# New orders and buffer numbers for seven of the nine instruction lists of an NSA and mLSTM decoder step

## The chip, the cores and the metric

The kernel runs on one core of a Trainium2 chip, in one launch. The metric is device time in microseconds (us). Five engines work side by side: TensorE (PE) multiplies matrices, VectorE (DVE), ScalarE (ACT) and GpSimd (POOL) work on elements, SyncE (SP) issues nearly all of the transfers; ACT issues a few. Each engine takes its instructions strictly in the order in which they stand in its list, and waits at an instruction until what it needs is done, so that everything behind it waits too.

## The reference

One inference step of a trunk of two layers, for a prompt of 512 tokens and eight sample sequences with one new token each (520 columns in all), in float32. Each layer adds to the residual what its mixer makes of the normed input:

```python
x = x + mixer_i(rmsnorm(x, w_i))          # i = 0: NSA attention, i = 1: mLSTM
out = W_out(mix(...) * silu(z))           # one input and one output projection for each mixer
```

Layer 0 is native sparse attention: keys and values are compressed by a small network (reading 1,024 cached rows for each sample through a page table), blocks are selected, and a window is attended, each branch with its own gate. Layer 1 is an mLSTM with four heads of 512 channels: a causal convolution, block-diagonal q, k and v, a stabilised matrix memory for each head that is updated and read, a norm for each head and the silu gate z. The outputs are the new hidden rows after a final norm, the new cache rows and windows, and the new memories (one 512 by 512 matrix for each head of each of the eight samples, and one for the prompt), normalisers, maxima and convolution rows.

## The kernel before

The 520 columns are worked in two chunks of 260. Every product with a weight is made of three matmuls with a split of both sides into a high and a low part (`mm3`, L761: high by high, high by low, low by high), so that a weight tile goes through three steps after its load: `load_w` (L777) issues the transfer of `wraw` on SP, ACT (in some places DVE) rounds it to `whi`, and POOL or DVE subtracts to get `wlo`. The first matmul of a tile needs `whi`, the third needs `wlo`.

Nothing is issued as the program text runs. The calls of all engines are recorded and then issued by lists of numbers that stand at the top of the file; that is why every row of the profile has the line L667, the one call in the helper. In the order of the program the lists are CALLS0 (projection to keys and values, compression), CALLS2 (projections to q and to the gate), ORDER0 (attention), CALLS1 (output projection of layer 0, norm of layer 1, projection `xm`, convolution and gates), ORDER1 (the projection `zm` to layer 1's gate, beside it the state steps of head 0), ORDER2 (the mLSTM cell with heads 1 to 3 and the output projection of heads 0 to 2) and CALLS3 (the output projection of head 3, the final norm, the outputs). Beside them MOVED tables name calls that go to another engine than the code says, and SLOTS gives each tile of a pool the number of its buffer. So the tables set the order in each engine's list; what then waits for what follows from the tiles. Pools that are closed hand their memory to later pools, and a load into the new pool waits for all users of the old tiles that lay there.

Four places matter below.

- The start. `x_t` (the input) and `nw` (norm factors, 12 KB) are loaded on ACT's queue, the weight `wraw` of the first projection and the small `b` on SP's. DVE scales this weight by `nw`, and PE's first matmul reads the scaled weight and `x_t`. Further on SP's load of a weight tile waits for a `wlo`, and sixteen cached pages (`praw`) stand behind it.
- The step from attention to the output projection. PE runs the projection as 24 matmuls for each of 8 tiles and 2 chunks, with the `uo` tiles (attention output, split) as moving side. The first two weights `w_o` are there early. SP then loads `x1` (the residual, from `in_xT`) into a pool that lies where attention's tiles lay; the next `w_o` stand behind it in SP's list.
- The end of ORDER1, `head_close` (L2284) for head 0: PE sums with ones over partitions (`t<-sd,ncs` and `t<-pr,ones`), DVE and ACT make a denominator `dn` and a numerator `nm`, DVE squares it to `pr`, and PE sums this. Beside it the last chunks of `zm` are evicted by DVE (`zt<-mm,rr`), and ACT makes their sigmoid (`zsg`, three passes).
- The tail, the output projection of head 3: DVE adds PE's sums to the residual (`x<-x,mm`), gates the head's output (`num<-num,zs`) and makes some of the `wlo` of the weights `in_m_out`.

Of the kernel before, what the change touches and what calls it, by code (L numbers as in the profile page):

```python
# [123 lines left out]
)  # L124
ORDER2 = (
# [42 lines left out]
)  # L168
CALLS0 = (
# [282 lines left out]
        0, 1, 0,  # L452
    ),
    ("fn", "w"): (
        0, 1, 2, 3, 4, 5, 6, 7, 8, 9, 10, 11, 12, 13, 14, 15, 16, 17, 18, 19, 0, 3, 2, 1, 13, 7, 10,
    ),
    ("fn", "sq"): (
        0, 1, 1, 1, 0, 1, 0, 1, 0, 1, 1, 1, 0, 1,
# [2627 lines left out]
```

## Time and profile before

| | us |
|---|---|
| median of 3 runs | 1004.49 (1002.74 to 1004.94) |
| the profiled execution | 1004.64 |
| its span, first to last instruction | 1002.9 |
| busy: PE | 977.8 |
| busy: DVE | 803.4 |
| busy: ACT | 554.9 |
| busy: POOL | 318.3 |

The profiled execution is 1.7 us longer than its span: that part lies outside of the instructions. PE is busy in 97% of the span. "Busy" is no proof that PE does useful work at its best rate, but here an idle stretch of PE and a stretch with a lower granted clock are the only visible losses, and they can be read window by window.

### The profile page before, as it was taken

Reading aid. Unit: us, or ns where it says so; the run is one execution under the profiler, and the core shown is the slowest. Engines: PE = TensorE matmul, PEld = TensorE weight load, DVE = VectorE, ACT = ScalarE, POOL = GpSimd, SP = SyncE. Lnnn points to the kernel's source line nnn. Section 1 sums busy time; section 2 is a strip of 40 time slices with the busy share of each in tenths; the row PEclk is TensorE's granted clock in tenths of the full one; section 3 lists DMA queues with packets and bytes.
Section 4 is the critical chain, followed back from the end, with each engine's and each line's share of the span. In section 5 each row is a group of like instructions: output and inputs, shape, how many; then the busy total and the mean of one; then the engine's idle time right before and its main releaser. Section 6 shows DMA issues by size and latency. Waiting matters only on the chain.

```text
span 1002.9 us, 22660 instructions
## 1 busy us (share of the span) xinstructions
PE 977.8 (97%) x8329; PEld 865.4 (86%) x8329; DVE 803.4 (80%) x1937; ACT 554.9 (55%) x1224; POOL 318.3 (32%) x389
## 2 busy tenths in 40 slices
PE   7999999999999999998999999999999999999998
PEld 5799999899988888788999997999676778777987
DVE  6988886776599988845787897957697899899986
ACT  6646443423588788723426654676566554654543
POOL 1123434431232435621133322243112332533330
PEclk9999999999999999998999999999999999999999
DMA  8755532335344534634644365688898789997733
GB/s 282 246 163 188 194 123 76 116 99 161 110 136 141 158 99 147 210 131 145 220 151 132 129 201 173 247 288 306 276 306 290 254 300 304 304 315 282 229 112 117
DMA packets 123681, 197.20 MB, mean 197 GB/s; under 512 B 16165, under 2 KB 64550, under 8 KB 123314
## 3 DMA queue, kind: packets, MB, share of 16 engines
q1 hardware_dynamic: 117954, 185.39, 56.8%
q10 hardware_dynamic: 5616, 10.36, 2.8%
q8 instruction: 65, 1.06, 0.4%
q14 instruction: 46, 0.38, 0.1%
HBM read 145.99 MB, written 58.10 MB: 203 GB/s over the span
## 4 chain that ended last, share of the span: by engine, by line
PE 83%; DVE 7%; DMA 3%; SPq 2%; ACT 2%; issue 2%; POOL 1%; DVEq 0%; ACTq 0%
PE mm L667 54%; PE s L667 12%; PE t L667 11%; PE d L667 6%; SPq L667 2%; DMA wraw<-in_w_kv 1%; DVE cs L667 1%; DMA wraw<-in_w_o 1%; DVE num L667 1%; DVE plo L667 1%; DVE wlo L667 1%; DMA dk<-in_cache 0%; DMA praw<-in_cache 0%; DMA wraw<-in_m_out 0%; ACT zsg L667 0%
## 5 line engine op out<-in xcount | busy, mean ns | idle before, releaser
L667 PE MATMUL mm<-hhi,whi 128*128 128x260 f32 x928 | 266.1, 287 | 0.2 <-DVE whi L667 0.2
L667 PE MATMUL mm<-hhi,wlo 128*128 128x260 f32 x928 | 262.7, 283 | 0.9 <-DVE wlo L667 0.8
L667 PE MATMUL mm<-hlo,whi 128*128 128x260 f32 x928 | 262.4, 283 | 0.0
L667 PEld LDWEIGHTS mm<-hhi,whi 128*128 128x128 f32 x928 | 174.8, 188 | 3.2 <-issue 1.5
L667 PEld LDWEIGHTS mm<-hhi,wlo 128*128 128x128 f32 x928 | 174.7, 188 | 1.3 <-DVE wlo L667 1.3
L667 PEld LDWEIGHTS mm<-hlo,whi 128*128 128x128 f32 x928 | 174.4, 188 | 1.1 <-issue 0.5
L667 POOL TENSOR_TENSOR wlo<-wraw,whi 128x512 fp32r<-128x512 f32 (+1 forms) x36 | 65.1, 1813 | 135.5 <-DVE whi L667 37.9
L667 DVE SCALAR_TENSOR_TENSOR cs<-t,wk,cs 128x512 f32<-128x512 f32 x128 | 88.8, 742 | 6.8 <-PE t L667 3.6
L667 DVE TENSOR_TENSOR wlo<-wraw,whi 128x1024 fp32r<-128x1024 f32 (+1 forms) x63 | 70.4, 1119 | 17.9 <-ACT whi L667 12.7
L667 ACT ACTIVATE cs<-cs,SBC 128x1024 f32<-128x1024 f32 x64 | 71.5, 1144 | 18.7 <-PE d L667 17.8
L667 ACT ACTIVATE whi<-wraw 128x1024 fp32r<-128x1024 f32 (+1 forms) x59 | 50.7, 864 | 51.8 <-DMA wraw<-in_m_out 14.3
L667 ACT ACTIVATE s<-s,mn 128x256 f32<-128x256 f32 (+3 forms) x128 | 70.5, 555 | 7.7 <-DVE mn L667 4.9
L667 POOL TENSOR_SCALAR s<-s,sm 128x256 f32<-128x256 f32 (+3 forms) x53 | 50.6, 965 | 54.2 <-DVE sm L667 27.5
L667 PE MATMUL mm<-uh,whi 128*128 128x260 f32 x224 | 65.6, 293 | 0.0
L667 PE MATMUL mm<-uh,wlo 128*128 128x260 f32 x224 | 63.4, 283 | 1.9 <-DVE wlo L667 1.9
L667 PE MATMUL mm<-ul,whi 128*128 128x260 f32 x224 | 63.3, 283 | 0.0
L667 DVE CUSTOM_DVE_ANT_0 s<-s,D 128x128 f32<-128x128 f32 (+3 forms) x128 | 58.3, 486 | 5.5 <-PE s L667 4.1
L667 PE MATMUL mm<-uo,whi 128*128 128x260 f32 x256 | 48.8, 293 | 3.8 <-ACT whi L667 3.8
L667 PE MATMUL s<-phi,w1a 128*128 128x256 f32 (+1 forms) x224 | 48.8, 296 | 0.0
L667 DVE TENSOR_TENSOR plo<-praw,phi 128x256 fp32r<-128x256 f32 (+1 forms) x50 | 39.3, 799 | 7.5 <-ACT phi L667 3.4
L667 PEld LDWEIGHTS mm<-uo,whi 128*128 128x128 f32 x256 | 41.5, 198 | 4.2 <-ACT whi L667 4.0
L667 PEld LDWEIGHTS mm<-uh,wlo 128*128 128x128 f32 x224 | 42.2, 188 | 2.1 <-DVE wlo L667 2.1
(503 smaller groups left out, 2571.0 us busy)
## 6 DMA issues: line engine op xcount, KB each, us to landing
cs<-in_state_C SPq DMA_DIRECT2D x64, 512.0 KB, 5.5
o_cs<-cs SPq DMA_DIRECT2D x64, 512.0 KB, 4.5
praw<-in_cache SPq DMA_DIRECT2D x128, 128.0 KB, 3.7
dk<-in_cache SPq DMA_DIRECT2D x128, 128.0 KB, 2.9
wraw<-in_m_in SPq DMA_DIRECT2D x32, 512.0 KB, 3.8
wraw<-in_m_out SPq DMA_DIRECT2D x32, 256.0 KB, 5.3
wraw<-in_w_kv SPq DMA_DIRECT2D x11, 512.0 KB, 3.9
wraw<-in_w_q SPq DMA_DIRECT2D x8, 512.0 KB, 3.4
```

The costliest lines, as they stand in the source:

```text
L667: return f(*[real(x) for x in a], **{n: real(x) for n, x in k.items()})
```

## The change

Only tables change; no function does. CALLS2, ORDER0, MOVED2 and the table of moved calls of ORDER0 stay as they are. CALLS0 differs in 257 of 892 places (up to place 130, and from 475 to 629), CALLS1 in 190 of 701 (the first 220), and ORDER1, ORDER2 and CALLS3 nearly everywhere. In the tables of moved calls, CALLS0 loses three calls and gains five, CALLS1 loses two and gains five, and ORDER1, ORDER2 and CALLS3 each exchange one. SLOTS gets other numbers for some fifteen kinds of tile. The two orders before and after, by their first lines:

```diff
 ORDER1 = (
-    0, 225, 226, 253, 227, 257, 15, 254, 1, 228, 230, 255, 2, 229, 231, 232, 233, 256, 8, 3, 259, 277, 16, 265, 262,
+    253, 0, 254, 257, 1, 2, 225, 226, 227, 15, 228, 229, 30, 274, 230, 231, 232, 233, 255, 265, 8, 3, 4, 256, 16, 5,
...
```

At the start ACT's list now begins with the load of `nw`, ahead of `x_t`; SP's begins with the three loads of the first weight, and the load of `b` stands behind the first cached pages; one of the scalings of this weight is POOL's instead of DVE's; the first rounding of the compression weight (`w1a`, 128x1024) stands behind the rounding `whi` of the projection's weight on ACT; the last load of `x_t` stands two roundings earlier.

The changed file is one line longer, so that L667 is L668 there. In the rows below a number after a name is the tile's own, so that the same name in the same row list means the same tile.

SP at the step from attention to the output projection, before (`dk` are the last rows of the window cache, `x1` is the residual, `wc0` and `wg` belong to layer 1's gates):

```order
L667 DMA dk_6588<-in_vwin 128x8x256
L667 DMA x1_6814<-in_xT 128x1040
L667 DMA wc0_6816<-in_w_qkv 128x192
L667 DMA wraw_6818<-in_w_o 128x1024
L667 DMA x1_6814<-in_xT 128x1040 x2
L667 DMA o_vwin<-in_vwin 16x8176
L667 DMA wraw_6875<-in_w_o 128x1024
L667 DMA wraw_6931<-in_w_o 128x1024
```

And of the change:

```order
L668 DMA dk_6588<-in_vwin 128x8x256
L668 DMA wraw_6789<-in_w_o 128x1024
L668 DMA wraw_6791<-in_w_o 128x1024
L668 DMA x1_6818<-in_xT 128x1040 x2
L668 DMA wc0_6821<-in_w_qkv 128x192
L668 DMA x1_6818<-in_xT 128x1040
L668 DMA wraw_6904<-in_w_o 128x1024
```

Two loads of `w_o` moved ahead of the first load of `x1`. The first of the two waits for a weight tile of a much earlier projection, the second for the `wlo` of the second `w_o` tile.

DVE at the end of ORDER1, before (`t_10326` holds PE's sums, `mm_10243` and `mm_10273` are the last two chunks of `zm`):

```order
L667 TENSOR_TENSOR zt_10315<-mm_10243,rr0_7464 128x260
L667 TENSOR_TENSOR zt_10315<-mm_10273,rr1_7543 128x260
L667 TENSOR_REDUCE dn_10349<-t_10326 128x16
L667 TENSOR_TENSOR dn_10349<-dn_10349,SBC_9038 128x16
L667 TENSOR_TENSOR dn_10349<-dn_10349 128x8
L667 TENSOR_TENSOR dn_10349<-dn_10349,SBC_9038 128x8
L667 RECIPROCAL dn_10349<-dn_10349 128x8
L667 TENSOR_TENSOR nm_10357<-VS_8690,dn_10349 128x32
L667 TENSOR_TENSOR nm_10357<-nm_10357,t_10326 128x32
L667 TENSOR_TENSOR pr_9150<-nm_10357 128x32
```

And of the change (`t_10151` holds the sums, `mm_10263` and `mm_10293` are the last two chunks):

```order
L668 TENSOR_REDUCE dn_10328<-t_10151 128x16
L668 TENSOR_TENSOR dn_10328<-dn_10328,SBC_9038 128x16
L668 TENSOR_TENSOR dn_10328<-dn_10328 128x8
L668 TENSOR_TENSOR zt_10258<-zt_10258,zsg1_10324 128x260
L668 TENSOR_TENSOR zt_10334<-mm_10263,rr0_7463 128x260
L668 TENSOR_TENSOR zt_10334<-mm_10293,rr1_7515 128x260
L668 TENSOR_TENSOR dn_10328<-dn_10328,SBC_9038 128x8
L668 RECIPROCAL dn_10328<-dn_10328 128x8
L668 TENSOR_TENSOR nm_10348<-VS_8690,dn_10328 128x32
L668 TENSOR_TENSOR nm_10348<-nm_10348,t_10151 128x32
L668 TENSOR_TENSOR pr_9144<-nm_10348 128x32
```

On PE the sums into `t` now stand 96 matmuls of `zm` earlier, and with them DVE's first three steps and ACT's step on `dn`, which ACT now does ahead of the last chunk's three sigmoid passes. The five DVE steps from the second product of `dn` to `pr` still stand behind the eviction of the last chunk.

DVE in the tail, before (`x` are residual tiles, `wlo_13139` is the low part of a tile of `in_m_out`):

```order
L667 TENSOR_TENSOR x23_11341<-x23_11341,mm_13051 128x260
L667 TENSOR_TENSOR x23_11341<-x23_11341,mm_13015 128x260
L667 TENSOR_TENSOR x22_11447<-x22_11447,mm_12960 128x260
L667 TENSOR_TENSOR x22_11447<-x22_11447,mm_12977 128x260
L667 TENSOR_TENSOR x24_11290<-x24_11290,mm_13066 128x260
L667 TENSOR_TENSOR x24_11290<-x24_11290,mm_13083 128x260
L667 TENSOR_TENSOR num_12919<-num_12919,zs_12949 128x512
L667 TENSOR_TENSOR num_12915<-num_12915,zs_12949 128x512
L667 TENSOR_TENSOR num_12794<-num_12794,zs_12949 128x512
L667 TENSOR_TENSOR wlo_13139<-wraw_13043,whi_13137 128x512
```

And of the change (`wlo_13121` is the tile that answers to it):

```order
L668 TENSOR_TENSOR x22_11581<-x22_11581,mm_12988 128x260
L668 TENSOR_TENSOR x23_11531<-x23_11531,mm_13004 128x260
L668 TENSOR_TENSOR x24_11284<-x24_11284,mm_13025 128x260
L668 TENSOR_TENSOR x24_11284<-x24_11284,mm_13042 128x260
L668 TENSOR_TENSOR num_12935<-num_12935,hy_12985 128x512
L668 SCALAR_TENSOR_TENSOR num_12935<-CT14_8840,par_7904,num_12935 128x512
L668 TENSOR_TENSOR wlo_13121<-wraw_13058,whi_13104 128x512
L668 TENSOR_TENSOR num_12935<-num_12935,zs_12920 128x512
L668 TENSOR_TENSOR num_13021<-num_13021,zs_12920 128x512
L668 TENSOR_TENSOR num_13019<-num_13019,zs_12920 128x512
```

The low part moved ahead of the three products with `zs`, and two of the six additions to `x` now come later; two other steps on `num` moved ahead of it.

## Rows read from the trace of the kernel before

**Rows 1.** The page's first part: busy time of each engine, its share of the span, its instructions.

```profile
PE 977.8 (97%) x8329; PEld 865.4 (86%) x8329; DVE 803.4 (80%) x1937; ACT 554.9 (55%) x1224; POOL 318.3 (32%) x389
```

**Rows 2.** Busy time by stretches of the span: the stretch, its length, the busy time of PE, of its weight loads, of DVE, ACT and POOL, then the granted clock of TensorE (1.00 is 2.4 GHz, 0.50 is 1.2 GHz), the share of the transfer engines and GB/s.

```profile
0.00:25.00 25.00, 17.71 (x89) 13.14 (x90) 17.42 (x33) 16.57 (x24) 3.12 (x7) 1.00 0.83 281
...
450.00:475.00 25.00, 20.90 (x149) 20.62 (x150) 12.56 (x21) 6.32 (x13) 4.51 (x3) 0.86 0.42 149
...
700.00:725.00 25.00, 22.61 (x198) 18.16 (x198) 15.89 (x50) 11.08 (x28) 5.43 (x12) 0.93 0.81 276
725.00:750.00 25.00, 25.00 (x164) 17.56 (x163) 22.82 (x52) 17.43 (x25) 4.46 (x9) 1.00 0.92 309
...
950.00:975.00 25.00, 22.55 (x185) 21.92 (x184) 21.37 (x50) 9.99 (x22) 7.26 (x8) 1.00 0.47 141
```

**Rows 3.** What PE waited for in the whole span: us in total, how often, the longest.

```profile
PE mm L667 <- DMA wraw<-in_w_kv: 7.2, 1, 7.2
PE mm L667 <- ACT whi L667: 3.8, 1, 3.8
PE mm L667 <- DVE wlo L667: 3.4, 3, 1.9
PE t L667 <- DVE pr L667: 2.4, 1, 2.4
```

**Rows 4.** The timeline of the first 24 us, from the lists of several engines (start, duration, engine, instruction, in brackets the idle time before it and what ended it; ACTq is ACT's issuing of transfers).

```profile
0.79 0.89 ACTq L667 DMA_DIRECT2D x_t<-in_xT  x2
1.71 0.45 ACTq L667 DMA_DIRECT2D nw<-in_norms  x1
...
8.52 0.73 ACT L667 ACTIVATE hhi<-x_t,nw 128x520 fp32r<-128x520 f32 x1 [0.61 <-DMA x_t<-in_xT]
...
6.64 0.49 DVE L667 TENSOR_TENSOR wraw<-wraw,nw 128x128 f32<-128x128 f32 x2 [6.64 <-DMA nw<-in_norms]
...
21.20 1.22 DVE L667 TENSOR_TENSOR wlo<-wraw,whi 128x1024 fp32r<-128x1024 f32 x1
...
7.19 2.10 PE L667 MATMUL mm<-x_t,wraw 128*128 128x260 f32 x4 [7.19 <-DMA wraw<-in_w_kv]
```

**Rows 5.** Transfers of the first 25 us: count, size of each, median us from issue to landing.

```profile
x_t<-in_xT ACTq DMA_DIRECT2D x2, 260.0 KB, 3.8
...
nw<-in_norms ACTq DMA_DIRECT2D x1, 12.0 KB, 4.8
```

**Rows 6.** The step to the output projection: one row of what SP waited for in the whole span, then the timelines of SP, ACT, DVE and PE from 436 to 456.

```profile
SPq L667 <- DVE uo L667: 18.6, 1, 18.6
...
440.77 0.34 SPq L667 DMA_DIRECT2D x<-in_xT  x1
...
443.72 11.27 SPq L667 DMA_DIRECT2D wraw<-in_w_o  x2
...
452.31 1.06 ACT L667 ACTIVATE whi<-wraw 128x1024 fp32r<-128x1024 f32 x1 [12.78 <-DMA wraw<-in_w_o]
...
435.97 1.22 DVE L667 TENSOR_TENSOR wlo<-wraw,whi 128x1024 fp32r<-128x1024 f32 x1
...
453.42 0.59 PE L667 MATMUL mm<-uo,whi 128*128 128x260 f32 x2 [3.80 <-ACT whi L667]
454.68 0.58 PE L667 MATMUL mm<-uo,wlo 128*128 128x260 f32 x1 [0.67 <-DVE wlo L667]
```

**Rows 7.** The end of ORDER1: the timelines of PE and DVE from 714 to 718.

```profile
714.04 0.44 PE L667 MATMUL t<-sd,ncs 128*32 128x8 f32 x32
714.31 0.32 PE L667 MATMUL t<-pr,ones 128*32 128x64 f32 x8
717.02 0.34 PE L667 MATMUL t<-pr,ones 128*32 128x32 f32 x8 [2.39 <-DVE pr L667]
...
714.14 0.43 DVE L667 TENSOR_TENSOR zt<-mm,rr 128x260 f32<-128x260 f32 x1 [1.51 <-PE mm L667]
...
716.06 0.17 DVE L667 TENSOR_TENSOR dn<-dn,SBC 128x8 f32<-128x8 f32 x1 [0.75 <-ACT dn L667]
...
716.78 0.19 DVE L667 TENSOR_TENSOR pr<-nm 128x32 f32<-128x32 f32 x1
```

**Rows 8.** Busy time by shorter stretches, with the columns of rows 2.

```profile
453.00:460.00 7.00, 5.90 (x26) 5.62 (x27) 4.12 (x6) 3.11 (x7) 0.00 (x0) 0.55 0.64 234
...
716.00:720.00 4.00, 2.98 (x18) 1.98 (x18) 3.00 (x17) 1.30 (x6) 0.55 (x2) 0.57 0.66 211
...
955.00:960.00 5.00, 4.24 (x35) 4.24 (x36) 4.83 (x11) 2.37 (x5) 0.76 (x2) 1.00 0.23 69
```

**Rows 9.** The tail: the timelines of DVE and PE from 951 to 957.

```profile
951.20 2.10 DVE L667 TENSOR_TENSOR x<-x,mm 128x260 f32<-128x260 f32 x6
953.22 1.89 DVE L667 TENSOR_TENSOR num<-num,zs 128x512 f32<-128x512 f32 x3
955.02 0.69 DVE L667 TENSOR_TENSOR wlo<-wraw,whi 128x512 fp32r<-128x512 f32 x1
...
956.35 0.75 DVE L667 SCALAR_TENSOR_TENSOR num<-CT,par,num 128x512 f32<-128x512 f32 x1
...
955.76 0.39 PE L667 MATMUL mm<-uh,wlo 128*128 128x260 f32 x1 [1.91 <-DVE wlo L667]
```

**Rows 10.** Transfers from 725 to 950 (a row of the state tiles' loads): count, size of each, median us from issue to landing.

```profile
cs<-in_state_C SPq DMA_DIRECT2D x41, 512.0 KB, 5.5
```

More of the change, by code (lines that the diff above doesn't have):

```diff
@@ L291 @@
 MOVED3 = (
-    2, 12, 16, 23, 27, 30, 31, 35, 65, 69, 120, 124, 141,
+    2, 7, 8, 12, 15, 20, 23, 27, 35, 37, 38, 45, 52, 65, 69, 85, 120, 124, 136, 143, 150,
 )
@@ L301 @@
 MOVEDP1 = (
-    1, 7, 12, 16, 17, 22, 31, 32, 47, 57, 61, 67, 82, 92, 97, 102, 106, 107, 117, 121, 127, 137, 147, 151, 162, 166,
-    172, 177, 181, 182, 196, 197, 211, 212, 230, 244, 246, 248, 328, 335,
+    1, 12, 16, 22, 27, 31, 32, 46, 57, 61, 62, 72, 77, 82, 87, 91, 92, 102, 107, 112, 117, 121, 132, 136, 137, 142,
+    147, 151, 166, 172, 177, 182, 187, 192, 196, 197, 202, 212, 225, 230, 244, 248, 255, 328,
 )
 MOVEDP2 = (
[5 rows of a table removed]
[5 rows of a table added]
 )
@@ L313 @@
     ("wstream", "w"): (
[6 rows of a table removed]
[6 rows of a table added]
     ),
     ("cmpw", "hs"): (
-        0, 1, 0, 1, 0, 0, 1, 0, 1, 0, 0, 1, 0, 1, 0,
+        0, 1, 0, 1, 0, 1, 0, 0, 1, 0, 0, 1, 0, 1, 0,
     ),
     ("ps", "bank"): (
[18 rows of a table removed]
[18 rows of a table added]
     ),
@@ L347 @@
     ("cmpw", "ph"): (
[3 rows of a table removed]
[3 rows of a table added]
     ),
     ("cmpw", "psm"): (
-        0, 1, 2, 2, 1, 0, 2, 1, 0, 2, 1, 0, 2, 1, 0, 2, 0, 1, 2, 1, 0, 1, 2, 1, 2, 0, 1, 0, 2, 1, 2, 1, 0, 1, 2, 2,
-        0, 1, 0, 1,
+        0, 1, 2, 2, 1, 0, 2, 1, 0, 2, 1, 0, 2, 1, 0, 2, 0, 1, 2, 1, 0, 1, 2, 2, 1, 0, 2, 2, 0, 1, 0, 1, 2, 1, 0, 0,
+        2, 1, 2, 1,
     ),
@@ L397 @@
     ("x1n", "sq"): (
-        0, 1, 0, 1, 0, 1, 0, 1, 0, 1, 0, 0, 1, 0,
+        0, 1, 0, 1, 0, 1, 1, 0, 0, 1, 0, 0, 1, 0,
     ),
@@ L402 @@
         29, 30, 31, 32, 33, 34, 35, 36, 37, 38, 39, 40, 41, 42, 43, 1, 0, 4, 2, 6, 5, 8, 9, 19, 22, 27, 25, 33, 31,
[4 rows of a table removed]
[4 rows of a table added]
+    ),
+    ("mi", "cv"): (
+        0, 1, 2, 3, 0, 3, 1, 3, 2, 3, 0, 3, 1, 0, 2, 1, 3, 1, 0, 1, 2, 0, 2, 1, 3, 2, 0, 3, 1, 3, 2, 1,
     ),
@@ L410 @@
     ),
-    ("mi", "cv"): (
-        0, 1, 2, 3, 0, 2, 3, 2, 1, 2, 0, 2, 3, 0, 1, 3, 2, 3, 0, 3, 1, 0, 1, 3, 2, 1, 0, 2, 3, 2, 1, 3,
-    ),
     ("st0", "cse"): (
-        0, 1, 2, 1, 2, 0, 1, 2, 0, 1, 2, 0, 2, 1, 0, 1, 2, 0, 1, 2, 0, 1, 2, 0, 0, 2, 1, 2,
+        0, 1, 2, 2, 1, 0, 1, 2, 0, 1, 2, 0, 1, 2, 0, 1, 0, 2, 1, 2, 0, 2, 1, 0, 1, 0, 2, 0,
     ),
@@ L423 @@
     ("zp", "zsg1"): (
-        0, 1, 1, 0, 1, 1, 1, 0, 0, 1, 1, 0, 1, 0, 1, 1, 0, 1, 1, 0, 0, 1, 0, 1, 1, 0, 1, 0, 1, 0, 1, 0,
+        0, 1, 1, 0, 1, 0, 1, 0, 1, 0, 0, 1, 0, 1, 0, 1, 0, 1, 0, 1, 1, 0, 1, 0, 0, 1, 1, 0, 1, 0, 1, 0,
     ),
     ("st", "cs"): (
-        0, 1, 2, 3, 3, 0, 1, 2, 3, 1, 2, 0, 2, 3, 0, 1, 3, 1, 2, 3, 0, 3, 1, 2, 0, 2, 3, 1, 2, 3, 0, 1, 2, 3, 1, 0,
+        0, 1, 2, 3, 0, 1, 2, 3, 2, 1, 0, 3, 0, 1, 2, 3, 1, 3, 0, 1, 2, 1, 0, 3, 0, 1, 2, 3, 0, 1, 2, 3, 0, 3, 1, 2,
     ),
@@ L434 @@
     ),
+    ("cella", "bd"): (
+        0, 1, 2, 3, 4, 5, 6, 0, 1, 3, 2, 4, 6, 3, 1, 2, 1, 5, 5, 5, 0, 4, 5, 6, 1, 2, 3, 5, 4, 0, 1, 6,
+    ),
     ("cella", "row"): (
-        0, 1, 2, 3, 4, 5, 6, 7, 8, 1, 5, 2, 0, 6, 7, 4, 8, 2, 3, 1, 0, 6, 4, 3, 2, 1, 7, 5, 0, 1, 6, 5, 7, 4, 8, 1,
-        3, 4, 2, 5, 6, 2, 4, 7, 1, 3, 8, 2, 5, 7, 5, 4, 6, 1, 4, 5, 3, 7, 5, 1, 0, 1, 8, 5, 3, 7, 8, 0, 1, 7, 3, 4,
-    ),
-    ("cella", "bd"): (
-        0, 1, 2, 3, 4, 5, 6, 0, 1, 2, 4, 3, 2, 1, 0, 4, 1, 0, 3, 1, 3, 2, 3, 5, 0, 4, 6, 3, 1, 2, 4, 0,
+        0, 1, 2, 3, 4, 5, 6, 7, 8, 3, 2, 1, 4, 7, 0, 3, 2, 1, 4, 5, 2, 3, 5, 4, 2, 3, 5, 4, 7, 3, 2, 4, 7, 1, 8, 3,
+        0, 1, 5, 2, 4, 5, 1, 7, 0, 3, 8, 1, 2, 7, 1, 4, 5, 0, 2, 4, 7, 3, 1, 5, 2, 6, 2, 4, 1, 7, 3, 4, 6, 5, 1, 3,
     ),
     ("cellb", "row"): (
-        0, 1, 2, 3, 4, 5, 0, 2, 1, 3, 5, 2, 1, 0, 4, 1, 2, 0, 3, 5, 4, 0, 2, 3, 1, 0, 2, 4, 5, 3, 0, 4, 3, 2, 1, 2,
-        4, 5, 3, 0,
+        0, 1, 2, 3, 4, 5, 2, 0, 1, 3, 4, 1, 0, 2, 5, 0, 3, 2, 1, 4, 5, 3, 2, 1, 0, 5, 4, 3, 2, 1, 4, 3, 1, 5, 0, 3,
+        1, 2, 4, 5,
     ),
     ("fw", "w"): (
-        0, 1, 2, 3, 4, 5, 1, 0, 2, 1, 0, 5, 3, 4, 0, 5, 3, 1, 2, 4, 5, 0, 1, 2, 4, 0, 5, 1, 4, 2, 0, 3, 4, 2, 5, 0,
-        1, 4, 2, 3, 5, 1, 0, 3, 2, 4, 0, 3, 1, 5, 2, 4, 3, 0, 2, 1, 0, 5, 3, 4, 2, 1, 3, 5, 0, 2, 4, 1, 3, 5, 4, 0,
-        2, 1, 5, 3, 0, 4,
+        0, 1, 2, 3, 4, 5, 1, 0, 3, 1, 5, 4, 2, 0, 1, 3, 2, 4, 5, 0, 3, 2, 1, 5, 0, 2, 3, 4, 2, 5, 0, 1, 4, 0, 3, 4,
+        0, 5, 2, 3, 1, 4, 3, 2, 0, 5, 4, 3, 0, 5, 1, 2, 3, 4, 0, 2, 4, 3, 0, 5, 1, 3, 2, 4, 0, 2, 4, 1, 5, 3, 0, 4,
+        2, 5, 3, 1, 0, 4,
     ),
@@ L454 @@
     ("fn", "w"): (
-        0, 1, 2, 3, 4, 5, 6, 7, 8, 9, 10, 11, 12, 13, 14, 15, 16, 17, 18, 19, 0, 3, 2, 1, 13, 7, 10,
+        0, 1, 2, 3, 4, 5, 6, 7, 8, 9, 10, 11, 12, 13, 14, 15, 16, 17, 18, 19, 0, 7, 5, 10, 3, 15, 13,
     ),
     ("fn", "sq"): (
-        0, 1, 1, 1, 0, 1, 0, 1, 0, 1, 1, 1, 0, 1,
+        0, 1, 1, 0, 1, 1, 0, 1, 1, 0, 0, 0, 1, 0,
     ),
```

321 rows, old and new, of tables (CALLS0, CALLS1, CALLS3, MOVED0) are left out of this document.

## The prediction

> **What bounds the kernel now.** I read four views in this order. The page's first part: PE is busy in 97% of the span, DVE in 80% [rows 1], so the time can fall only where PE waits or is slowed. The busy time by stretches of 25 us: nearly all show PE at 25.00 of 25 with the granted clock at 1.00, as 725 to 750 does; the reader is to see the four that don't [rows 2]. PE stands 7.29 us in the first stretch, 4.10 in that from 450, 2.39 in that from 700, 2.45 in that from 950. Two of them also show a lower clock: 0.86 over 25 us is 0.14 x 25 = 3.5 us of full-rate work lost, 0.93 is 0.07 x 25 = 1.75. Then the list of PE's waits, which names the four holes: the first weight 7.2, `whi` 3.8, `wlo` 3.4 in three waits (the longest 1.9), `pr` 2.4 [rows 3]. Last the timelines around each, for the chain behind it. I call them holes A (start), B (output projection), C (end of ORDER1) and D (tail). Elsewhere PE has nothing to gain from another order; it can only lose there.
>
> **Hole A.** PE starts at 7.19. DVE scales the first weight at 6.64, when `nw` lands, and `nw` was issued at 1.71, behind two loads of `x_t` [rows 4]: 4.9 us on the way, as its own row says (4.8) [rows 5]. Now it is issued first, where `x_t` stood, at 0.79. If its way stays 4.9 us, all moves by 1.71 - 0.79 = 0.9. If it is as quick as the first loads of `x_t`, 3.8 us [rows 5], it lands at 4.6; `x_t`, one issue of 0.45 later, lands at 0.79 + 0.45 + 3.8 = 5.0, and PE gains some 2.1. I take 1.5, between the two. Downstream the start feeds a `wlo` that ends at 21.20 + 1.22, and SP's sixteen pages wait for this tile; ACT's work on the third `x_t` waited for its transfer until 8.52 [rows 4], and that load is issued when it was. If this transfer sets the later steps, nothing is left of the gain: the bound below is 0.
>
> [...]
>
> **Hole B.** SP's load of `x1` stands until 440.77, after 18.6 us of waiting for the last `uo`, and the next `w_o` loads stand behind it; the pair issued from 443.72 reaches ACT at 452.31, 8.6 us later, and PE waits 3.80 for `whi` and 0.67 for `wlo`, 4.47 us [rows 6]. Then the clock is low: 0.55 over 453 to 460 [rows 8], half rate for most of it, the 3.5 us above. In the new order the two loads stand ahead of `x1`. The first waits only for a tile of long before. The second waits for the `wlo` that DVE ends at 435.97 + 1.22 = 437.2 [rows 6]; even with the 8.6 us it lands at 445.8, and with `whi` (1.06) and `wlo` (1.22) it is ready at 448.1. PE's wait began at 453.42 - 3.80 = 449.6, where it wants the first of the two; the second comes 48 matmuls later. So both are in time, and `x1` is not held up, since 437.2 lies before 440.77. What PE needs next, later `w_o` tiles, stands behind `x1` as before, from some 442 on; each has 48 matmuls of time. B gives 4.47 + 3.5 = 8.0. The bounds are 0, if something else is late at 449.6, and 8.0.
>
> **Hole C.** PE ends its `zm` matmuls at about 714.1, runs the sums (714.04 to 714.63), and starts on `pr` only at 717.02 [rows 7]. The chain between is DVE's eviction of the last chunk, three sigmoid passes on ACT with the step on `dn` behind them, and DVE's steps from 716.06 to 716.97. Now the sums and DVE's first steps lie 96 matmuls earlier, and ACT does its `dn` step before the last passes. But DVE's five steps still stand behind the last eviction. So PE waits for 0.43 (eviction, from 714.14) and 716.97 - 716.06 = 0.91 of steps, with the gaps 1.4 us, against 2.39: 1.0 less. The clock: after the 2.39 wait it was 0.57 over 716 to 720; after the wait of 1.91 in the tail it stayed 1.00 over 955 to 960 [rows 8]. A wait of 1.4 is nearer to the second, so I take no fall and 1.75 more. C gives 2.75; the bounds are 0 and 2.39 + 1.75 = 4.1.
>
> [...]
>
> **Hole D.** DVE works without a gap: six additions to `x`, three products with `zs` (1.89), then the `wlo` at 955.02 for which PE waits 1.91 [rows 9]. Now `wlo` stands ahead of the three products and of two additions (2.10 / 6 = 0.35 each), but behind two other steps on `num` (0.75 for one [rows 9], about 0.63 for the other, a third of 1.89). Net 1.89 + 0.70 - 1.38 = 1.2 us earlier. D gives 1.2, bounds 0 and 1.91.
>
> **Everything else.** The same number of matmuls runs, and in the dense stretches DVE, POOL and SP have other orders under a full PE. That cover is thin in places: the state steps from 725 run with the transfer engines at 0.92 [rows 2], and in ORDER2 and the tail some of DVE's steps now stand only a dozen of PE's instructions ahead of their use. Before, waits below a microsecond were what such closeness cost, and rows 3 holds all that mattered. I charge 1.0 for new small waits; the bounds are 0 and what the fourth rival below says.
>
> **Sum.** 1.5 + 8.0 + 2.75 + 1.2 - 1.0 = 12.4. The profiled execution took 1004.64, its span 1002.9 with 1.7 outside, which the change doesn't touch. 1004.64 - 12.4 = 992.2. The median of the runs shown is 1004.49, so the same sum from there gives 992.1; the runs spread from 1002.74 to 1004.94.
>
> **Rivals.**
> 1. Only hole B goes. For it: A's gain is lost to the third `x_t`, C keeps its clock fall, D's list is dense. Against: C's and D's shortening follow from steps with measured durations. 1004.64 - 8.0 = 996.6.
> 2. Hole B is only halved. The early loads share the transfer engines with the last cache windows, or ACT or DVE comes to `whi` and `wlo` late behind `uo`; PE waits for half of 4.47 and the clock falls all the same. B is then worth 2.2, and 1004.64 - (1.5 + 2.2 + 2.75 + 1.2 - 1.0) = 998.0. Against it: the first load has some 20 us (SP stood at `x1` for 18.6).
> 3. Nothing shows. All gains are given back in small waits under the dense stretches: 1004.6. For it only that nearly every list is new; against it 12 us of small waits, where the kernel before had under 3 outside of the four holes.
> 4. Slower. In ORDER2 SP's list holds the loads of state tiles behind stores (`zd` at the end of ORDER1, then `o_cs`), each waiting for a DVE step; a load takes 5.5 us [rows 10] with the transfer engines at 0.92 [rows 2], and PE's sums over a head's tiles (`d<-cs`) come late by one load in heads 1, 2 and 3. With a clock fall of 1.75 each, 3 x (5.5 + 1.75) = 21.8, and 1004.64 - 12.4 + 21.8 = 1014.0. It decides from 12.4 / 3 - 1.75 = 2.4 us of lateness for each head. For it: the high share. Against: before, the same loads and stores under the same share let PE run 25.00 of 25 [rows 2].
>
> **How the numbers follow.** The four holes as summed 0.55; rival 1 0.2; rival 2 0.1; rival 3 0.05; rival 4 0.1. The forecast is the likeliest, 992.2. With all upper bounds, 2.1 + 8.0 + 4.1 + 1.9 = 16.1, the time is 988.5, and a run can lie 1 us below; so 987.5 below. Above, the range takes in rivals 1 and 2 with a few more small waits, to 1001; what is left out is rivals 3 and 4 and little else. A difference under 0.2% (2 us) is about what a measurement of this kernel cannot tell from none. Faster than that: 0.55 + 0.2 + 0.1 = 0.85; within it 0.05; slower 0.1.
>
> **What would show it.** A: PE's first matmul at 5.1 to 6.3, and the `wlo` near 21.2 earlier by as much. B: no wait of PE for `whi` near 445 to 450, SP's `w_o` loads issued before `x1`, and a clock of 1.00 through the following 25 us. C: a wait for `pr` of 1.2 to 1.6 and a clock of 1.00 after it. D: a wait for `wlo` under 1 us. Elsewhere PE at 25.00. Wrong would be a wait for `whi` of over 2 us at B, a clock below 0.95 in any stretch, or PE idle by more than 1 us in one stretch of heads 1 to 3.

## The result and the profile after

| | us |
|---|---|
| before, median of 6 runs of this comparison | 1003.62 (1001.97 to 1008.53) |
| after, median of 6 runs | 997.16 (995.11 to 999.03) |
| ratio | 0.9928, 95% interval 0.9902 to 0.9954 |
| the profiled execution after, and its span | 999.03, 996.5 |

The kernel became faster by 6.5 us in the median. The forecast was 12.4 us of gain, to 992.2, with a range of 987.5 to 1001.0: the direction and the range held, half of the gain did not come. The profiled execution is the slowest of the six after. One correction to the section on the change: CALLS1 gains four moved calls, not five, and ORDER1, ORDER2 and CALLS3 exchange more than one: 12, 46 and 4 numbers leave their tables and 16, 41 and 12 enter. So more work goes to POOL, which is busy 336.3 us after against 318.3 before.

The page's first part after, which answers to [rows 1]:

```profile
PE 973.9 (98%) x8329; PEld 860.4 (86%) x8329; DVE 797.8 (80%) x1922; ACT 556.0 (56%) x1224; POOL 336.3 (34%) x404
```

The busy time by stretches of 25 us after (columns as in [rows 2], the clock third from the end):

```profile
0.00:25.00 25.00, 18.68 (x97) 13.62 (x98) 18.23 (x32) 16.61 (x24) 4.28 (x8) 1.00 0.85 290
150.00:175.00 25.00, 23.02 (x174) 22.11 (x175) 16.89 (x25) 7.60 (x15) 10.65 (x8) 1.00 0.20 65
450.00:475.00 25.00, 25.00 (x211) 25.00 (x210) 17.47 (x28) 9.10 (x21) 7.56 (x6) 1.00 0.52 181
700.00:725.00 25.00, 22.69 (x133) 14.50 (x132) 20.12 (x57) 13.99 (x30) 9.05 (x17) 1.00 0.91 289
850.00:875.00 25.00, 23.66 (x186) 18.92 (x186) 16.71 (x42) 19.43 (x34) 11.47 (x10) 1.00 0.92 318
...
950.00:975.00 25.00, 23.79 (x191) 22.94 (x190) 20.59 (x44) 9.49 (x24) 12.42 (x13) 1.00 0.26 81
```

Hole B is closed, and the clock is at 1.00 in every stretch. But the stretches from 150 and from 850, full before, have holes now. PE's waits after, by what ended them, against [rows 3]:

```profile
PE d L668 <- DMA x_t<-in_xT: 5.7, 2, 5.0
PE s L668 <- DVE plo L668: 3.5, 3, 2.7
PE mm L668 <- DVE wlo L668: 1.4, 2, 0.8
PE t L668 <- DVE VB L668: 1.3, 1, 1.3
PE t L668 <- DVE pr L668: 1.3, 1, 1.3
PE mm L668 <- POOL wlo L668: 1.0, 2, 0.9
...
PE mm L668 <- DVE cs L668: 0.7, 1, 0.7
...
PE mm L668 <- DVE bdm L668: 0.6, 1, 0.6
```

`whi` is gone, `pr` is 1.3 instead of 2.4. New are `plo` with 2.7 in one wait, `VB` with 1.3, `cs`, `bdm` and one of 0.9 for a `wlo` from POOL. The largest new one lies near 152. Timeline of the compression there, after (start, duration, engine, step; in brackets the idle time before it and what ended it):

```profile
147.17 0.69 DVE L668 TENSOR_TENSOR psm<-praw 128x512 f32<-128x512 f32 x1 [0.71 <-DMA praw<-in_cache]
147.78 0.88 DVE L668 SCALAR_TENSOR_TENSOR hs<-hs,hcst,hsg 128x636 f32<-128x636 f32 x1
148.25 2.59 POOL L668 TENSOR_TENSOR plo<-praw,phi 128x1024 fp32r<-128x1024 f32 x1 [2.34 <-ACT phi L668]
148.57 3.35 DVE L668 TENSOR_TENSOR plo<-praw,phi 128x1024 fp32r<-128x1024 f32 x1
...
151.98 0.38 PE L668 MATMUL s<-plo,w1a 128*128 128x256 f32 x1 [2.71 <-DVE plo L668]
```

DVE's `plo` takes 3.35 us where the same step takes 1.22 elsewhere. It starts 0.32 us after POOL's, and ends 1.08 after it, so that nearly all of its usual 1.22 came when POOL was done. The same is seen in ORDER2, where two steps of DVE on a few columns take 1.22 us each, and each ends 0.01 to 0.03 us after a POOL step:

```profile
868.43 1.28 POOL L668 TENSOR_TENSOR wlo<-wraw,whi 128x512 fp32r<-128x512 f32 x1 [1.69 <-DVE wlo L668]
868.52 1.22 DVE L668 TENSOR_TENSOR dn<-dn,SBC 128x16 f32<-128x16 f32 x1
869.71 1.27 POOL L668 TENSOR_TENSOR acc<-acc,sq 128x512 f32<-128x512 f32 x1
869.77 1.22 DVE L668 TENSOR_TENSOR dn<-dn 128x8 f32<-128x8 f32 x1
871.03 0.68 DVE L668 TENSOR_TENSOR VB<-t,VB 8x512 fp32r<-8x512 f32 x1
...
871.76 0.50 PE L668 MATMUL t<-VB,OH 128*128 128x512 f32 x1 [1.34 <-DVE VB L668]
```

So a step of DVE with two inputs in SBUF (the memory that holds the tiles) waits for the rest of a POOL step that began before it. I name this theory P. The Trainium skill has the rule on its page "SBUF — State Buffer", section "Who interferes with whom": a VectorE instruction with two SBUF inputs contends with a GpSimd instruction that reads SBUF, the port pair that they share is an exclusive lock, and the order of issue decides who blocks. The trace agrees, 1.22 us for a step of 0.17. It is the rule that the prediction should have weighed and did not.

The trace of before has a control for P. I took DVE's tensor-tensor steps that begin inside a POOL tensor step and by the usual time of their form would end before it. Of those with an input in PSUM (where PE leaves its sums, the tiles `t`, `mm`, `s` and `d`) all 68 keep their usual time and end first. Of those with both inputs in SBUF 39 of 49 end after the POOL step; the other ten lie beside POOL's `plo<-xp,phi`, which is itself stretched there, to 0.67 to 1.65 us where the shortest of its kind take 0.31 to 0.34.

The rivals of P: each part of the change is worth what I forecast, and the loss comes from somewhere else (F); the lists set these waits in every execution (L); DVE's list is simply too full there (Q).

### The profile page after: what moved, and what is told of

The parts are those of the page before. It is cut to its first block, busy times and chain, and to the rows that moved or that the text cites. A ratio compares the mean times of both kernels' runs of the same rounds, so it can differ in the third digit from the quotient of the medians.

```text
span 996.5 us, 22671 instructions
## 1 busy us (share of the span) xinstructions
PE 973.9 (98%) x8329; PEld 860.4 (86%) x8329; DVE 797.8 (80%) x1922; ACT 556.0 (56%) x1224; POOL 336.3 (34%) x404
## 4 chain that ended last, share of the span: by engine, by line
PE 86%; DVE 8%; ACT 2%; DMA 2%; issue 1%; SPq 1%; POOL 0%; ACTq 0%; DVEq 0%; POOLq 0%
PE mm L668 55%; PE s L668 14%; PE t L668 12%; PE d L668 6%; DMA x_t<-in_xT 1%; DVE plo L668 1%; SPq L668 1%; DVE num L668 1%; DVE cs L668 1%; DMA praw<-in_cache 1%; DVE wlo L668 1%; DVE dn L668 0%; DVE x L668 0%; DVE ul L668 0%; ACT zsg L668 0%
## 5 line engine op out<-in xcount | busy, mean ns | idle before, releaser
L668 PE MATMUL mm<-hhi,whi 128*128 128x260 f32 x928 | 266.5, 287 | 0.2 <-DVE whi L668 0.2
L668 PE MATMUL mm<-hhi,wlo 128*128 128x260 f32 x928 | 262.4, 283 | 1.4 <-DVE wlo L668 1.4
L668 PE MATMUL mm<-hlo,whi 128*128 128x260 f32 x928 | 262.0, 282 | 0.0
L668 PEld LDWEIGHTS mm<-hhi,whi 128*128 128x128 f32 x928 | 174.7, 188 | 3.2 <-ACT zsg L668 0.8
L668 PEld LDWEIGHTS mm<-hhi,wlo 128*128 128x128 f32 x928 | 174.7, 188 | 1.9 <-DVE wlo L668 1.8
L668 PEld LDWEIGHTS mm<-hlo,whi 128*128 128x128 f32 x928 | 174.7, 188 | 1.1 <-issue 0.5
L668 POOL TENSOR_TENSOR wlo<-wraw,whi 128x512 fp32r<-128x512 f32 (+1 forms) x34 | 63.2, 1861 | 150.4 <-ACT whi L668 47.2
L668 DVE SCALAR_TENSOR_TENSOR cs<-t,wk,cs 128x512 f32<-128x512 f32 x128 | 88.5, 743 | 16.7 <-ACT cs L668 14.6
L668 DVE TENSOR_TENSOR wlo<-wraw,whi 128x1024 fp32r<-128x1024 f32 (+1 forms) x65 | 74.4, 1145 | 10.7 <-ACT whi L668 6.9
L668 ACT ACTIVATE whi<-wraw 128x1024 fp32r<-128x1024 f32 (+1 forms) x60 | 51.8, 868 | 54.7 <-PE mm L668 31.6
L668 ACT ACTIVATE cs<-cs,SBC 128x1024 f32<-128x1024 f32 x64 | 71.2, 1140 | 9.4 <-PE d L668 9.4
L668 ACT ACTIVATE s<-s,mn 128x256 f32<-128x256 f32 (+3 forms) x128 | 70.5, 555 | 7.6 <-DVE mn L668 4.9
L668 POOL TENSOR_SCALAR s<-s,sm 128x256 f32<-128x256 f32 (+3 forms) x53 | 50.6, 965 | 53.5 <-DVE sm L668 26.8
L668 PE MATMUL mm<-uh,whi 128*128 128x260 f32 x224 | 64.9, 290 | 0.7 <-DVE cs L668 0.7
L668 PE MATMUL mm<-uh,wlo 128*128 128x260 f32 x224 | 63.6, 284 | 1.0 <-POOL wlo L668 1.0
L668 PE MATMUL mm<-ul,whi 128*128 128x260 f32 x224 | 63.2, 282 | 0.0
L668 DVE CUSTOM_DVE_ANT_0 s<-s,D 128x128 f32<-128x128 f32 (+3 forms) x128 | 58.3, 486 | 5.5 <-PE s L668 4.0
L668 PE MATMUL s<-phi,w1a 128*128 128x256 f32 (+1 forms) x224 | 49.1, 297 | 0.0
L668 DVE TENSOR_TENSOR plo<-praw,phi 128x256 fp32r<-128x256 f32 (+1 forms) x50 | 41.3, 836 | 7.6 <-ACT phi L668 3.4
L668 PE MATMUL mm<-uo,whi 128*128 128x260 f32 x256 | 46.2, 283 | 0.0
L668 PEld LDWEIGHTS mm<-uh,whi 128*128 128x128 f32 x224 | 42.1, 188 | 2.4 <-DVE cs L668 0.8
L668 PEld LDWEIGHTS mm<-uh,wlo 128*128 128x128 f32 x224 | 42.1, 188 | 1.7 <-POOL wlo L668 1.4
```

The costliest lines, as they stand in the source:

```text
L668: return f(*[real(x) for x in a], **{n: real(x) for n, x in k.items()})
```

## The experiments

All are made of the two kernels' tables; their files are nine or ten lines shorter, so that the helper's line is L658. Where a list is taken from the other kernel, a tile that lives on from the list before keeps its buffer.

**One part alone, four times.** The kernel before with the tables of one part taken from the change:

```diff
 e1_start:     CALLS0
-    4, 22, 5, 2, 6, 1, 8, 15, ...
+    1, 4, 5, 7, 6, 9, 8, 13, ...
 e2_outproj:   CALLS1
-    15, 4, 0, 64, 28, 5, 16, 9, ...
+    15, 28, 44, 4, 0, 1, 64, 16, ...
 e3_head0:     ORDER1
-    0, 225, 226, 253, 227, 257, 15, 254, ...
+    253, 0, 254, 257, 1, 2, 225, 226, ...
 e4_cell_tail: ORDER2 and CALLS3
-    290, 291, 315, 2, 327, 3, 341, 292, ...
+    2, 291, 315, 294, 318, 290, 1, 5, ...
```

> The kernel before with CALLS0 (its order, its moved calls and its buffer numbers) taken from the change; all other lists as before. Theory P (shared port): the start itself gains 1.2 us (first matmul at 5.0 instead of 7.2, then a wait of 0.8 for the second x_t), and the shifted phase lets POOL's plo begin just ahead of DVE's plo near 148, so that DVE stands behind it and PE waits 2.7 us near 152: together about 1.4 us slower than before, 1005 to 1006, and no other new wait. Rival F (the forecast's term): the start is worth 1.5 us and the wait near 152 belongs to other lists; 1.5 us faster, no wait above 1 us near 152.

> The kernel before with CALLS1 alone taken from the change. Both theories: the waits for whi and wlo near 450 (4.5 us) go, the clock stays at 1.00 from 450 to 475, and the time falls by 8.0 us, to 995.5 to 997. Rival (half of the hole): the two early weights collide with the last cache rows when the start is not 1.4 us later too, a wait for whi of over 1 us is left and the gain is under 5 us.

> The kernel before with ORDER1 alone taken from the change. Theory P: PE's wait for pr falls from 2.39 to about 1.3, the clock stays near 1.00 from 716 on, but PE still waits for bdm behind pr, since the steps of DVE and ACT from pr to bdm take as long as before; worth 0.8 to 1.0 us in all. Rival F (the forecast's term): 1.0 for the wait and 1.75 for the clock, 2.75 us faster.

> The kernel before with ORDER2 and CALLS3 alone taken from the change. Theory P: four or five waits of 0.4 to 1.3 us for dn, cs, wlo and ul from 870 on, each with a DVE or POOL instruction stretched to about 1.3 us beside one of the other engine; together 2 to 3 us slower than before. Rival F (the forecast's terms): the wait of 1.91 in the tail falls by 1.2 and the small new waits cost under 1.0, so 0.2 to 1.2 us faster.

The ratios to before: 0.9985 (0.9970 to 1.0000) for e1, 0.9913 (0.9885 to 0.9941) for e2, 0.9984 (0.9967 to 1.0000) for e3, 1.0026 (1.0006 to 1.0045) for e4. To see where, I read the start of the same numbered matmuls of PE (8,329 in every run, the first is number 0) from each trace. The first two columns of the table are starts, the others the time from one numbered matmul to the other, in us:

| run | 1st starts | 250th starts | 750 to 1000 | 4000 to 4250 (hole B) | 5500 to the last |
|---|---|---|---|---|---|
| before | 7.19 | 53.60 | 34.54 | 37.33 | 380.75 |
| e2_outproj | 6.03 | 52.25 | 34.55 | 29.71 | 380.43 |
| e3_head0 | 6.09 | 52.19 | 34.55 | 36.77 | 379.83 |
| e4_cell_tail | 6.31 | 52.41 | 34.55 | 36.66 | 383.62 |
| e1_start | 5.81 | 53.69 | 34.57 | 37.19 | 380.13 |
| after | 4.97 | 52.60 | 37.45 | 29.62 | 382.08 |
| f0_again | 4.80 | 52.05 | 38.91 | 29.72 | 381.76 |
| f1_plo_dve | 5.12 | 52.42 | 35.31 | 29.71 | 381.08 |
| f2_vb_first | 4.98 | 51.85 | 34.47 | 29.71 | 380.78 |
| f4_all | 8.08 | 53.95 | 34.78 | 29.62 | 378.49 |
| g1_head0 | 6.25 | 51.93 | 34.61 | 29.62 | 377.82 |
| g2_new_start | 4.96 | 52.85 | 34.47 | 29.72 | 377.73 |

Hole B is worth 6.9 to 7.7 us in every run that has the new CALLS1, a little under the 8.0 of the expectation. e2 has no other new list, and its median, 995.36, lies 8.3 us below the 1003.64 of the kernel before beside it: this one part gives as much as the whole change.

In e1 theory P missed: it wanted a slower kernel and a wait of 2.7 near 152. The ratio is 1.5 us of gain, with an interval that ends at 1.0000, and no wait near 152 appeared, with the very lists that the changed kernel has up to there. Both are as F had them, but not for its reason: the first matmul came at 5.81, the 250th at 53.69, later than in any run with the old start but f4's, so the start gained nothing in this trace. Timeline of e1 at that place:

```profile
148.15 0.88 DVE L658 SCALAR_TENSOR_TENSOR hs<-hs,hcst,hsg 128x636 f32<-128x636 f32 x1
148.94 1.22 DVE L658 TENSOR_TENSOR plo<-praw,phi 128x1024 fp32r<-128x1024 f32 x1
149.24 3.17 POOL L658 TENSOR_TENSOR plo<-praw,phi 128x1024 fp32r<-128x1024 f32 x1 [2.20 <-ACT phi L658]
```

Here DVE's `plo` begins 0.30 us ahead, takes its 1.22, and POOL's pays, with 3.17 where it took 2.59 after. In both traces DVE's steps before it waited for a page's transfer, and POOL's `plo` for ACT's `phi`, which had waited for PE: a race.

e3 is worth about 0.6 us (379.83 against 380.13 to 380.75 with the old lists there), below what theory P gave and far from 2.75. e4 loses 3.2 us (383.62 against a mean of 380.44), a little over what theory P gave; three of its waits, with the same causes and nearly the same sizes as after:

```profile
PE t L658 <- DVE VB L658: 1.3, 1, 1.3
...
PE mm L658 <- POOL wlo L658: 1.0, 2, 0.9
...
PE mm L658 <- DVE cs L658: 0.9, 1, 0.9
```

**The change again, and one cause taken away at a time.**

```diff
 f0_again:    (nothing)
 f1_plo_dve:  MOVED0
-816
 f2_vb_first: ORDER2
-    762, 816, 179, 190, 564,
+    762, 816, 190, 179, 564,
```

> The changed kernel, once more and with nothing changed, for a second profile. Theory R (a race): whether DVE's plo or POOL's plo near 148 begins first hangs on when the transfers at the start landed; in the run with CALLS0 alone DVE's came first by 0.30 us and PE did not wait, in the first profile of the changed kernel POOL's came first by 0.32 and PE waited 2.7. So this profile shows one of the two and nothing between: DVE's plo takes either 1.2 or over 3 us, and PE's 1000th matmul stands 2.5 to 3 us apart accordingly; the waits at 871, 931, 956 and 962 (1.3, 0.7, 0.4, 0.9) come again in any case, since there every engine follows PE. Rival L (the lists): the wait near 152 belongs to the order and comes again, 2.7 us, in every execution.

> The changed kernel with one call moved: POOL's plo at 148.25 (the one that ran beside DVE's plo of 3.35 us) is done by DVE, directly behind its own in the list. Theory P (one engine waits for the whole instruction of the other): both plo take 1.2 us on DVE, PE waits under 0.8 us near 152 and never more, and the kernel gains up to 2 us where the wait was there. Rival Q (DVE's queue is too long there, since the pages come 0.8 us later): one instruction more on DVE makes the wait longer, 3.5 to 4 us.

> The changed kernel with one step of ORDER2 moved: VB (whose wait of 1.34 us PE shows at 871.76) stands ahead of the three steps on dn instead of behind them in DVE's list; POOL's wlo and acc stay where they are. Theory P: the products of dn still take 1.2 us each beside POOL, but VB, which reads one side from PSUM, takes 0.68 beside POOL's wlo, and PE's wait is gone; 1.3 us faster from there on. Rival Q (DVE is too full there, whatever the order): a wait of 0.5 to 1.3 stays, or comes for the next tile within 10 us.

f0 gave 0.9909 (0.9877 to 0.9940), with the race lost again: DVE's `plo` 3.35, 0.32 us behind POOL's. It alone does not part R from L; e1 and f2 do, whose CALLS0 is the same and whose stretch from 750 to 1000 is 34.5. So theory R holds in its main point: of the four profiles with these lists unchanged two lost the race, for 2.9 and 4.4 us, and two did not. The 4.4 lies outside of R's 2.5 to 3, and that the landing of the first transfers decides is not shown: the 250th matmul starts at 52.60 and 52.05 where the race was lost, at 53.69 and 51.85 where it was won. The waits are alike (2.71 and 2.69), but in f0 the clock fell behind the wait, to 0.93 in the stretch from 150, where it stayed at 1.00 after:

```profile
150.00:175.00 25.00, 23.62 (x167) 22.71 (x168) 15.47 (x24) 6.76 (x14) 10.03 (x8) 0.93 0.19 65
```

f1 gave 0.9916 (0.9883 to 0.9949). Its times are no better than those of f0 (median 997.07 against 995.98), so only the trace speaks here. With POOL's `plo` gone from beside it (it is done on DVE at 152.05, one step later than I had written), DVE's takes 1.22 again and PE waits 0.60, under the 0.8 of theory P and far from the 3.5 of Q:

```profile
148.40 1.22 DVE L658 TENSOR_TENSOR plo<-praw,phi 128x1024 fp32r<-128x1024 f32 x1
...
149.67 0.39 PE L658 MATMUL s<-plo,w1a 128*128 128x256 f32 x1 [0.60 <-DVE plo L658]
```

f1's trace holds a second race, which nobody arranged. PE's wait for `cs` (0.70 at 931.09 after, there also in e4, f0 and f2) is missing in it. After, and in f1:

```profile
926.72 1.30 POOL L668 TENSOR_TENSOR wlo<-wraw,whi 128x512 fp32r<-128x512 f32 x1 [8.39 <-DVE dn L668]
926.76 1.30 DVE L668 TENSOR_TENSOR dn<-dn,SBC 128x16 f32<-128x16 f32 x1
...
925.76 0.18 DVE L658 TENSOR_TENSOR dn<-dn,SBC 128x16 f32<-128x16 f32 x1
926.03 1.30 POOL L658 TENSOR_TENSOR wlo<-wraw,whi 128x512 fp32r<-128x512 f32 x1 [8.65 <-DVE dn L658]
```

Behind POOL's `wlo` the step on `dn` takes 1.30, ahead of it 0.18, and DVE's `cs` stands behind `dn`.

f2 gave 0.9902 (0.9867 to 0.9937). `VB` goes first, and no wait for it is left; `dn` still stands behind POOL, and nobody waits for that:

```profile
864.86 0.68 DVE L658 TENSOR_TENSOR VB<-t,VB 8x512 fp32r<-8x512 f32 x1
864.91 1.27 POOL L658 TENSOR_TENSOR wlo<-wraw,whi 128x512 fp32r<-128x512 f32 x1 [1.70 <-DVE wlo L658]
...
866.18 1.28 POOL L658 TENSOR_TENSOR acc<-acc,sq 128x512 f32<-128x512 f32 x1
866.25 1.24 DVE L658 TENSOR_TENSOR dn<-dn 128x8 f32<-128x8 f32 x1
...
866.34 0.79 PE L658 MATMUL t<-VB,OH 128*128 128x512 f32 x1
```

From the 7,400th to the 7,500th matmul, where this wait stood, f2 takes 16.52 us and the three with the old place of `VB` 18.12 to 18.14. From the 5,500th on it takes 380.78, those three 381.08 to 382.08: 0.3 to 1.3 less, 0.9 in the mean, so part of it is given back.

**A faster version.** Four edits on the changed kernel:

```diff
-CALLS0, MOVED0 of the change
+CALLS0, MOVED0 of before
 ORDER2: 190 ahead of 179, as in f2
-    731, 248, 274, 849, ... 446, 267, 270, 260,
+    731, 248, 849, ... 446, 267, 270, 274, 260,
 MOVED3
-23
```

> The changed kernel with CALLS0 of before, VB ahead of dn as in the run with that step alone, the steps on dn of the next head (near 926) behind the two pairs of cs in DVE's list, and one wlo of the tail (for which PE waits 0.85 at 962) done by DVE instead of POOL. Theory P: no wait near 152, at 871, 931 and 962; the sum from the changed kernel's first profile is 2.5 + 1.3 + 0.7 + 0.8 = 5.3 us less, a profiled time near 993 and a median near 992. Rival Q: the waits come back elsewhere on the same stretch of DVE's list, and the median stays above 995.

It gave 0.9875 (0.9843 to 0.9907), median 992.77, where the expectation was near 992; f0, run beside it, had 995.98, and all four runs of f4 lie below all four of f0. None of the four waits is left, and the end takes 378.49, 3.2 us less than the mean of 381.64 of the three runs without these edits. Then the place behind `zm` (g1), and the new start on top of it (g2):

```diff
 g1_head0: ORDER1
-    337, 207, 208, 215, 220, 216, 338, 221, 339, 340, 194, 346, 222, 341, 247, 334, 209, 342, 343, 345,
+    337, 338, 207, 208, 215, 216, 339, 220, 340, 341, 221, 342, 194, 346, 222, 343, 247, 334, 209, 345,
 g2_new_start: the same, with
-CALLS0, MOVED0 of before
+CALLS0 of the change, MOVED0 as in f1
```

> The kernel of the run with all four edits, and in ORDER1 the steps to pr moved ahead: ACT's step on dn stands ahead of the last two rounds of sigmoid passes, DVE's five steps to pr ahead of the eviction of the last chunk of zm, DVE's steps behind pr directly behind that eviction, and ACT's root directly behind the last sigmoid passes. Theory P (the chain through pr to bdm bounds this place, not the clock): the wait for pr (1.33) goes, the wait for the second pair of bdm (0.61) goes, that for POOL's bdm stays or grows to about 1; from the end of zm to the first d<-cs it is 1.0 to 1.7 us shorter than with the four edits alone. Rival Q (something else on DVE or ACT is late there): under 0.5 us is gained, since PE waits as long for the next tile.

> The same with CALLS0 of the change instead of that of before, and POOL's plo near 148 done by DVE, so that the race there is gone. Forecast's term for the start: 1.5 us faster than with the start of before. Theory S (the start is set by when the first transfers land, which differs by some 2 us from one execution to the next, in either order): the medians of the two agree within 1 us.

g1 gave 0.9905 (0.9889 to 0.9922), median 993.44; g2 0.9895 (0.9878 to 0.9911), median 992.64. These and f4 can't be told apart by their times. By the trace g1's end takes 377.82, 0.7 less than f4's, and from the end of `zm` to the first `d<-cs` it is 5.20 against 6.05: the waits of 1.33, 0.35 and 0.61 went, and one of 1.73 took their place, since POOL's `bdm` stands behind a copy of `zt` that needs the last sigmoid:

```profile
705.35 0.43 DVE L658 TENSOR_TENSOR zt<-zt,zsg 128x260 f32<-128x260 f32 x1 [0.81 <-ACT zsg L658]
...
705.84 0.19 POOL L658 COPY ZSS<-zt 128x8 f32<-128x8 f32 x1 [1.94 <-DVE zt L658]
...
705.99 0.40 POOL L658 TENSOR_TENSOR bdm<-cst,mw 128x128 f32<-128x128 f32 x1
...
706.45 1.98 PE L658 MATMUL mm<-CT,bdm 128*128 128x512 f32 x4 [1.73 <-POOL bdm L658]
```

So the chain to `bdm` bounds that place, as theory P said, but the gain is under its 1.0. The medians of g1 and g2 are 0.8 us apart, as theory S said; but with intervals of 1.7 us to either side the times do not rule out 1.5 us for the start. The traces say more, below.

## Why the prediction was half right

- **Hole A: the step was sized from one late execution.** It took 7.19 for PE's start [rows 4]. The five other runs with the old start show 6.03 to 8.08. That `nw` would come earlier was right: DVE scales the first weight at 3.30 after, at 6.64 before. PE then waits for `x_t`, begins 1.6 us earlier in the mean of six against six, and loses it again, after to the second `x_t` (0.76) and to `wlo` (0.59). The 250th matmuls start at 52.72 in the mean of the six with the old start, at 52.58 with the new: worth 0.1, with a 95% interval of 1.0 to either side, instead of 1.5. So the bound of 0 that I gave was nearer; between it and the smaller value of 0.9 these traces do not decide.
- **Hole B: right.** Both waits gone, the clock at 1.00, 6.9 to 7.7 us against 8.0.
- **Hole C: the wait was right, its worth and the price of the clock were not.** PE waits 1.33 for `pr` (forecast 1.4), and the clock is 1.00 behind it. But "I take no fall and 1.75 more" counted a low clock over a stretch in which PE had little to do. After:

```profile
708.06 0.27 PE L668 MATMUL t<-pr,ones 128*32 128x32 f32 x8 [1.33 <-DVE pr L668]
...
709.71 1.12 PE L668 MATMUL mm<-CT,bdm 128*128 128x512 f32 x2 [0.36 <-POOL bdm L668]
...
711.11 0.28 DVE L668 TENSOR_TENSOR bdm<-cst,mw 128x128 f32<-128x128 f32 x1
711.31 1.50 DVE L668 COPY QZ<-QKS 128x8 f32<-128x8 f32 x4
711.45 1.12 PE L668 MATMUL mm<-CT,bdm 128*128 128x512 f32 x2 [0.62 <-DVE bdm L668]
```

  From the sums on `pr` to the last `bdm` that PE waits for, DVE and ACT need 3.05 us (708.06 to 711.11). PE's few matmuls fit under that at either clock. e1 shows it cleanly: the same lists and the same wait of 2.4 as before, but a clock of 1.00, where [rows 2] has 0.93:

```profile
700.00:725.00 25.00, 21.87 (x193) 16.87 (x192) 16.93 (x52) 12.27 (x30) 4.74 (x12) 1.00 0.82 278
```

  and from the 6,000th to the 6,500th matmul it is only 0.35 us faster than before: so much for the 1.75. Nor did the shorter wait give its 1.0. From the 6,000th matmul to PE's first `d<-cs` e3 takes 41.42, and e1 and e2, with the old lists and the clock at 1.00, 41.65 and 41.79. What lies between `pr` and that matmul grew from 3.95 to 4.43. C is worth 0.6 in all (42.00 before), not 2.75.
- **Hole D and everything else: D gave more than I said, the charge of 1.0 was too small.** The wait of 1.91 [rows 9] is gone whole in every run with the new ORDER2 and CALLS3 (the two for DVE's `wlo` that are left in the list after lie at 21 and 184); I had 1.2. The 0.85 at 962 is another one, 100 matmuls later, for a `wlo` that POOL makes beside DVE's casts:

```profile
960.38 1.57 POOL L668 TENSOR_TENSOR wlo<-wraw,whi 128x512 fp32r<-128x512 f32 x1 [2.61 <-DVE whi L668]
...
962.00 0.39 PE L668 MATMUL mm<-uh,wlo 128*128 128x260 f32 x1 [0.85 <-POOL wlo L668]
```

  Against the gain stand `VB` 1.34, `cs` 0.70, this 0.85 and smaller ones: ORDER2 and CALLS3 together lose 3.2 us in e4, where I had a gain of 0.2. From PE's first `d<-cs` to its last matmul e4 takes 279.8, the changed kernel 279.0 to 280.0 (after, f0, f1), the runs with the old lists 277.2 to 277.6. In e4 and after about 1 us of that is idle time of PE; the rest is busy time of PE, 276.2 to 276.5 against 274.8 to 274.9, and what stretches it is in the main not shown. One piece goes with a neighbour again: the four copies to `QZ` take 1.50 us beside POOL's `vl` after (the line at 711.31 above) and 0.39 in f0, and from the first `d<-cs` to the 6,504th matmul after takes 0.75 us more than f0. I wrote that small waits below a microsecond were what closeness cost; a DVE step behind a POOL step costs up to 1.3 here, however short it is. No more of this happens than before: I added up over each trace what DVE's steps beside a POOL step take beyond the usual time of their form, some 58 us before and 56 after. What the new order changed is which of these steps PE waits for.
- **Not foreseen: the race at 148.** It costs 0 or 2.9 to 4.4 us from one execution to the next, and the profiled one lost it. f0's other three runs lie at 995.61 to 996.00, 4.4 below its profiled one, as if they had won it; there is no trace of them.
- **Outside of the span.** I took 1.7 us there as untouched. The profiled execution after has 2.5, the six runs 1.7 to 2.8, the runs of the kernel before beside the experiments at most 1.8. What adds to it stays open.
- **Two readings.** The four holes are not the only stretches short of 25.00: that from 25 has 23.23 before, that from 175 has 23.92. All of PE's waits outside of the holes come to 5.5 us, not under 3. Neither enters the sum.
- **The rivals.** Rival 1, 996.6, came nearest to 997.16: in the sum little but B is left. Of its reasons the start holds in part (lost again, after to the second `x_t` rather than the third), and the clock fall at C does not. Rival 2 fell with B. Rival 4 fell: the longest wait for a load of `cs` in any run is 0.22 us (f0).

The terms for the profiled execution, against the mean of the runs with the old lists at each place: to the 750th matmul 0.6 gained, the race 2.9 lost, 1000 to 4000 0.4 gained, B 7.4, 4250 to 5500 0.8, the rest 1.6 lost: 4.7 in all, 7.6 where the race is won, both without what lies outside of the span. The median gain of 6.5 lies between.

## What to carry to other kernels

Before an order of instructions is judged by its dependencies, look in the trace for DVE steps that take far more than the usual time of their form and end with a POOL step, or just behind one: that is the price of a neighbour, here on steps with both inputs in SBUF and on some copies and casts, and an order that puts such a step ahead of what PE waits for pays it. Move what PE waits for ahead of it, or one of the two to another engine. A low clock costs time only where PE has work to do in that stretch (0.35 us of 1.75 at `pr`, about 1.5 at 152, where f0 stands against after), and a start that is set by the first transfers has to be read from several executions before it is priced.

## What the runs showed that I had not expected

- Two engines whose steps cannot run side by side make one program take two courses: 0.32 us behind costs DVE 2.1 us, 0.30 ahead costs it nothing.
- The clock does not follow the length of a wait alone: behind the wait of 2.4 for `pr` the stretch shows 0.93 before and in e4, and 1.00 in e1 and e2; behind the wait of 2.7 at 152 it shows 1.00 after and 0.93 in f0. What decides stays open.
- With the same lists the first matmul started between 6.03 and 8.08 us (old start), and between 4.80 and 5.81 (new start).
